# Out-projection tiles in half-row pairs, earlier weight pieces on GpSimd, and a sample product from split pieces

## The chip, the cores and the metric

The kernel runs on one core of a Trainium2 chip. The metric is the device time of one execution in microseconds (us); the median of three executions of the kernel before is 1808.09 us (1805.63 to 1809.71). Engines are named as in the profile: PE is TensorE, PEld its weight loads, DVE VectorE, ACT ScalarE, POOL GpSimd, SP the engine that issues most transfers (DMAs).

## The reference, cut to what matters

One layer of a decoder, for a prompt of 1024 tokens and for 64 sample tokens (8 sequences of 8) that share the weights. Three branches (differential attention, a pooling mixer, memory attention) are merged; then come the steps that this case is about:

```python
    x = x + merged @ w_out
    f, conv_state = conv_ffn(rmsnorm(x, norm2_g), conv_prefix.astype(x.dtype), w_ffn_gate, w_ffn_up,
...
def conv_ffn(h, prefix, w_gate, w_up, conv_w, conv_b, w_down):
    L = h.shape[1]
    g = h @ w_gate
    u = h @ w_up
    ext = jnp.concatenate([prefix, g], axis=1)
    gc = conv_b
    for j in range(CONV_WIDTH):
        gc = gc + conv_w[j] * ext[:, j:j + L]
    f = (jax.nn.gelu(gc) * u) @ w_down
    return f, ext[:, ext.shape[1] - (CONV_WIDTH - 1):]
```

w_out is 1024 x 1024, the gate and up weights 1024 x 2816, w_down 2816 x 1024, and CONV_WIDTH is 3; f is added to x and a last norm follows.

All data are float32. The merge, the projections and the attention ahead of this are the same in both kernels.

## The kernel before, in words

**Numbers in two pieces.** A float32 matrix is split into a high piece (a cast to TensorE's fast float32 form, by ACT, line 109) and a low piece (the rest, by DVE or GpSimd, line 110). A product is then three matmuls: high by high, high by low, low by high. One piece of a weight tile `wA` to `wD` holds 4 x 128 rows by 128 columns; a matmul here is 128x128 by 128x512 and covers 512 tokens.

**The out-projection** (lines 938 to 995) works in two column halves (nb = 0, 1) of 512 columns. In each, the 64 sample rows come first (line 195), then eight tiles of 128 tokens, 24 matmuls a tile (line 187), into the PSUM tag `nat` (two buffers). DVE adds the result to x1 (line 925), ACT squares the sum into the same PSUM tile and sums it (line 926), which frees it. x1 and x1s are loaded for this with DMAs that SP issues (lines 948 and 950). In the second half, a tile is complete: it is normalised (lines 930 and 932, with some small DVE operations of lines 116 to 122) and transposed for the feed-forward part, four 128x128 transposes at a time (line 106, function `put`), into PSUM buffers `tp` and `av` in turn, then split by ACT and DVE.

**Seven products instead of eight.** The feed-forward product of a 256-column weight block with 1024 tokens is done in the manner of Strassen and Winograd: tokens and the rows of x fall in two halves each, and seven products of half size, with sums on both sides, give the result. The token side is B11, B21, B22 (plain) and T1 to T4 (sums and differences). The token halves are the even and the odd tiles: B11 is made of x1[0], x1[2], x1[4], x1[6], and the differences combine x1[2a] with x1[2a+1]. The results therefore go back to token order through strided views (`hv`, `q`).

**The weight blocks.** m runs over 22 blocks, even ones of the gate and odd ones of the up weight. `prep(m)` makes the weight pieces: wA from a11 and a12, wB from s1 and s2, wC from s3 and s4, wD from a22; the sums s1 to s4 are made by GpSimd into buffers `stm` (lines 1080, 1084, 1093, 1097). `products(m)` runs the seven products, 12 matmuls each (line 1108): B11 by wA, T1 by wB, T2 by wB, B21 by wA, T3 by wC, B22 by wC, T4 by wD, into the two halves a and b of a tile `big` (two PSUM banks, two such tiles) and a tile `nat`; ACT copies and DVE adds (line 1124) collect them in SBUF tiles `gu` (six buffers). `prep(m + 1)` is emitted between the products of m. For the sample rows, `sample_ffn` multiplies xs (64 columns wide) with the raw float32 weight: eight products, two rows of the trace each, two at a time side by side in the array (line 1031). The results are transposed (line 106), and in gate blocks convolved (lines 1022 to 1024).

**What sets the order.** The kernel is emitted in program order and then each engine's queue is arranged by a scheduler that works with its own estimates; on the chip each engine runs its queue strictly in that order, and an instruction waits for its operands and for the release of the buffer that it writes. A PSUM tile `big` is released as a whole, both halves. After the feed-forward loop the down projection follows (lines 1174 and on): its matmuls are lines 1221 (prompt) and 1228 (sample, from the split tile `fs`).

Of the kernel before, what the change touches and what calls it, by code (L numbers as in the profile page):

```python
# [32 lines left out]
def hybrid_step(ctx, tc, x_prompt, x_sample, mem_prompt, cache_k, cache_v, page_table, state_pool,  # L33
# [867 lines left out]
    pB_cm = tc.tile_pool(name="pB", bufs=1, reuse_waits="tile")  # L901
    pB = pB_cm.__enter__()
    B11, B21, B22 = [pB.tile([P, 2, 4, 512], F32R, name=f"B{i}") for i in ("11", "21", "22")]

# [9 lines left out]

    with tc.tile_pool(name="p5", bufs=1, reuse_waits="tile") as p5:
        x1 = [p5.tile([P, D], F32, name=f"x1_{t}") for t in range(NT)]
        x1s = p5.tile([TS, D], F32, name="x1s")
        g2b = p5.tile([P, D], F32, name="g2b")
        nc.sync.dma_start(g2b, bc(norm2_g[0], P))
# [13 lines left out]

        def put(Bt, xh, a):
            pt = tpb()
# [5 lines left out]
        raws = {}  # L941
        T1 = T2 = None
        todo, late = [], []
        for nb in range(2):
            n0 = nb * 512
            wf = load_w(cols(w_out, n0))
            if nb == 0:
                nc.sync.dma_start(x1s, x_sample)
                for t in range(NT):
                    nc.sync.dma_start(x1[t], x_prompt[t * P:(t + 1) * P])  # L950
            else:
                raws[0], raws[1] = raw_ffn(0), raw_ffn(1)
            pt = nat()
            mm_s(pt, wf, ms)
            add_sq(x1s, (pt[0:TS], pt[TS:P]), pt[0:TS], TS, NT, nb)
            if nb == 1:
                nc.gpsimd.dma_start(x1s_d, x1s)
                norm2(x1s, TS, NT)
                xs = ap_.tile([P, KT, P], F32, tag="hs", bufs=1, name="xs")
                pt = tpb()  # L960
                for k in range(KT):
                    tr(pt[:, k * TS:(k + 1) * TS], x1s[:, k * P:(k + 1) * P])
                nc.scalar.copy(xs[:, :, 0:TS], pt.rearrange("p (k t) -> p k t", k=KT))
            for i, t in enumerate((0, 2, 1, 3, 4, 6, 5, 7) if nb else range(NT)):
                pt = nat()
# [6 lines left out]
                if i == 3:  # L972
                    T1, T2 = [ap_.tile([P, 2, 4, 512], F32R, tag="act", bufs=4, name=f"T{q}") for q in (1, 2)]
                a = t // 2
                if t % 2 == 0:
                    put(B11, x1[t][:, 0:512], a)
                    put(B21, x1[t][:, 512:D], a)
                    continue
                xa, xb = x1[t - 1], x1[t]
                put(B22, xb[:, 512:D], a)  # L980
                nc.vector.tensor_tensor(xa[:, 0:512], xb[:, 0:512], xa[:, 0:512], op=ALU.subtract)
# [15 lines left out]
    with tc.tile_pool(name="fa", bufs=1, reuse_waits="tile") as fa:  # L997
# [11 lines left out]
        def gu():  # L1009
            return fa.tile([P, T], F32, tag="gu", bufs=6, name=f"gu{uid()}")  # L1010
# [282 lines left out]
```

## Time and profile before

| what | value |
| --- | --- |
| median of three executions | 1808.09 us (1805.63 to 1809.71) |
| the profiled execution | 1810.49 us, its span 1808.7 us |
| mean granted clock of TensorE | 0.987 |
| busy: PE, DVE, ACT, POOL | 1739.5, 899.2, 717.2, 391.7 us |

The span is the time from the first to the last event of the profile. In the order of time a row reads: start, duration from first to last instruction of the group, engine, line, operation, output and inputs, shapes, count, and in brackets the idle time of that engine before it and what ended it. Matmuls are pipelined, so the cadence of a group is the distance of its start to the next start. The granted clock says at what share of its full speed TensorE ran.

### The profile page before, as it was taken

The numbers are of one execution on the slowest core, as the hardware profiler recorded it, in microseconds if no ns is written. First come the engines' busy times: TensorE is split into PE (matmuls) and PEld (weight loads), VectorE is DVE, ScalarE is ACT, GpSimd is POOL, SyncE is SP. The second block draws the span as 40 slices with busy tenths as digits, with TensorE's granted clock in tenths as the row PEclk, the third lists the DMA queues.
The fourth block names the chain that finished last, engine by engine and source line by source line (L and its number), as shares of the span: only waits on it lengthen the run. The fifth ranks groups of instructions, "written<-read, shape, count | busy, mean of one in ns | idle before, by whom it ended". The sixth has DMA issues, their size and how long they took to land.

```text
span 1808.7 us, 22927 instructions
## 1 busy us (share of the span) xinstructions
PE 1739.5 (96%) x8285; PEld 1334.1 (74%) x8285; DVE 899.2 (50%) x1543; ACT 717.2 (40%) x1396; POOL 391.7 (22%) x427
## 2 busy tenths in 40 slices
PE   7999999998999999999989899999999999999997
PEld 5887876764666777767767677777777777888876
DVE  6411134230221666677716676666666666336464
ACT  5321235331222666665413343333333334234343
POOL 1113020301101324112201344444444442000000
PEclk9999999999999999999989899999999999999999
DMA  7441251468565323154432222222222223646563
GB/s 276 139 142 66 83 183 38 135 187 266 195 230 178 96 79 117 56 193 161 145 122 88 49 72 71 71 71 71 71 71 71 71 71 135 226 145 217 197 229 109
DMA packets 137367, 234.74 MB, mean 130 GB/s; under 512 B 25679, under 2 KB 71533, under 8 KB 137253
## 3 DMA queue, kind: packets, MB, share of 16 engines
q1 hardware_dynamic: 122117, 187.16, 32.5%
q0 software_dynamic: 15136, 46.12, 6.8%
q8 instruction: 65, 1.06, 0.2%
q14 instruction: 49, 0.40, 0.1%
HBM read 182.74 MB, written 50.54 MB: 129 GB/s over the span
## 4 chain that ended last, share of the span: by engine, by line
PE 82%; issue 7%; DVE 4%; DMA 3%; ACT 2%; POOL 1%; SPq 1%; POOLq 0%; ACTq 0%; DVEq 0%
PE nat L178 17%; PE big L1108 17%; PE big L1221 10%; PE nat L1108 7%; PE nat L187 6%; PE big L178 4%; PE nat L1221 3%; PE tp L1031 3%; PE tp L106 3%; PE av L106 2%; PE av L804 2%; PE big L774 2%; PE nat L195 2%; PE av L542 1%; PE big L523 1%
## 5 line engine op out<-in xcount | busy, mean ns | idle before, releaser
L178 PE MATMUL nat<-act,hl 128*128 128x512 f32 x1344 | 357.7, 404 | 0.0
L178 PEld LDWEIGHTS nat<-act,hl 128*128 128x128 f32 x1344 | 242.1, 189 | 61.0 <-issue 14.0
L187 PE MATMUL nat<-hl,act 128*128 128x512 f32 x768 | 186.6, 401 | 10.1 <-ACT nat L926 8.3
L1221 PE MATMUL big<-wd,fh 128*128 128x512 f32 x792 | 187.4, 390 | 4.1 <-ACT big L1189 2.5
L187 PEld LDWEIGHTS nat<-hl,act 128*128 128x128 f32 x768 | 146.5, 193 | 42.3 <-ACT nat L926 8.7
L1221 PEld LDWEIGHTS big<-wd,fh 128*128 128x128 f32 x792 | 148.3, 188 | 36.3 <-ACT big L1189 3.4
L1108 PE MATMUL big<-B,wA 128*128 128x512 f32 x528 | 130.5, 395 | 0.1
L110 DVE TENSOR_TENSOR hl<-raw,hl 128x1024 fp32r<-128x1024 f32 x52 | 66.4, 1287 | 123.8 <-ACT hl L109 112.8
L110 DVE TENSOR_TENSOR wd<-wr,wd 128x1024 fp32r<-128x1024 f32 x66 | 84.5, 1282 | 74.1 <-ACT wd L109 68.2
L1108 PEld LDWEIGHTS big<-B,wA 128*128 128x128 f32 x528 | 97.4, 188 | 28.2 <-ACT gu L1133 8.3
L109 ACT CAST wd<-wr 128x1024 fp32r<-128x1024 f32 x66 | 69.3, 1052 | 83.3 <-PE tps L1228 35.3
L110 DVE TENSOR_TENSOR wB<-stm,wB 128x512 fp32r<-128x512 f32 x44 | 50.4, 1147 | 73.6 <-ACT wB L109 73.6
L568 POOL DMA_DIRECT2D gl<-ev x48 | 26.2, 546 | 277.5 <-ACT ev L567 253.2
L567 ACT COPY ev<-nat 128x512 f32<-128x512 f32 x48 | 28.1, 586 | 112.7 <-PE nat L178 106.9
L1108 PE MATMUL nat<-B,wC 128*128 128x512 f32 x264 | 69.9, 399 | 0.0
L109 ACT CAST hl<-raw 128x1024 fp32r<-128x1024 f32 x60 | 62.6, 1053 | 16.3 <-PE nat L178 8.2
L1162 POOL TENSOR_TENSOR gu<-gu,gu 128x1024 f32<-128x1024 f32 x22 | 57.0, 2591 | 52.2 <-DVE gu L1124 22.5
L1221 PE MATMUL nat<-wd,fh 128*128 128x512 f32 x264 | 67.1, 389 | 0.0
L1108 PE MATMUL big<-T,wD 128*128 128x512 f32 x264 | 66.8, 401 | 0.0
L1097 POOL TENSOR_TENSOR stm<-rf,stm 128x512 f32<-128x512 f32 x22 | 28.6, 1299 | 169.8 <-DVE wB L110 169.8
L1108 PE MATMUL big<-T,wC 128*128 128x512 f32 x264 | 64.6, 393 | 0.0
L1108 PE MATMUL nat<-T,wB 128*128 128x512 f32 x264 | 64.1, 390 | 0.0
(419 smaller groups left out, 3080.3 us busy)
## 6 DMA issues: line engine op xcount, KB each, us to landing
wr<-in_w_ffn_down SPq DMA_DIRECT2D x66, 512.0 KB
raw<-in_w_in SPq DMA_DIRECT2D x40, 512.0 KB
kr<-in_cache_k SPq DMA_DIRECT2D x64, 256.0 KB
vr<-in_cache_v SPq DMA_DIRECT2D x64, 256.0 KB
gl<-ev POOLq DMA_DIRECT2D x48, 256.0 KB, 3.0
rf<-in_w_ffn_gate SPq DMA_DIRECT2D x22, 512.0 KB
rf<-in_w_ffn_up SPq DMA_DIRECT2D x22, 512.0 KB
f_d<-gu POOLq DMA_DIRECT2D x22, 512.0 KB, 3.0
```

The lines of the kernel that those rows point to most:

```text
L106: nc.tensor.transpose(out, in_, ident[:n, :n])
L109: nc.scalar.copy(hi, src)
L110: (lo_eng or nc.vector).tensor_tensor(lo, src, hi.bitcast(F32), op=ALU.subtract)
L178: nc.tensor.matmul(out, wf(k, pw)[:, n0:n0 + P], acts[c][ph][:, k, :], start=(k == ks[0] and (pw, ph) == (0, 0)), stop=(k == ks[-1] and (p ...
L187: nc.tensor.matmul(out, acts[c][ph][:, k, o:o + P], wf(k, pw), start=(k == ks[0] and (pw, ph) == (0, 0)), stop=(k == ks[-1] and (pw, ph) = ...
L195: nc.tensor.matmul(out, stack[:, k, :], wf(k, pw), start=(k == ks[0] and pw == 0), stop=(k == ks[-1] and pw == 1))
L774: nc.tensor.matmul(S[:, k0:k0 + n], Qd[:, m, part, qs], Kst[:, m, k0:k0 + n], start=(part == 0), stop=(part == 1))
L804: nc.tensor.matmul(av[:, :P], aT[:, k * P:(k + 1) * P], vn[:, k0 + k], start=(k0 + k == 0), stop=(k0 + k == i))
L1031: nc.tensor.matmul(pt[r:r + TS, 0:256], xs[:, k, 0:TS], raw[k // 4][:, k % 4], start=(k < 2), stop=(k >= 6), tile_position=(0, r))
L1108: nc.tensor.matmul(out, wt[:, pw, k], Bt[:, ph, k], start=(start and k == 0 and (pw, ph) == (0, 0)), stop=(k == 3 and (pw, ph) == (1, 0)), ...
L1162: nc.gpsimd.tensor_tensor(g[i], g[i], gts[i], op=ALU.mult)
L1221: nc.tensor.matmul(banks[i][nb], fh[:, ph, kk, i * P:(i + 1) * P], wh[:, pw, nb * 512:(nb + 1) * 512], start=(k == 0 and (pw, ph) == (0, 0 ...
```

## The change

1. **Token halves in a row.** The two token halves are now tiles 0 to 3 and 4 to 7: B11 is made of x1[0] to x1[3], the differences combine x1[a] with x1[a+4]. The products' results are 512 contiguous tokens, and the strided views are gone.
2. **Out-projection.** Two tiles share one `big` tile, a half each (the sample rows take a half of one too), instead of a `nat` each. Tiles go in the order 0 to 7 in both column halves. The transposes of a tile (`ops_of`) are emitted two tiles behind its projection and take their PSUM buffers from `nat` and from `tp`/`av` in turn, four buffers in all. The four subtractions of a tile pair are all on GpSimd (lines 1115, 1116, 1120, 1121), but for the last pair, where two stay on DVE.
3. **Transfers.** x1s and x1 are loaded ahead of the norm weights g2b and of the first feed-forward weights.
4. **First two weight blocks.** For m = 0 and 1, the low pieces are made by GpSimd, and the sums s1 to s4 in place in the raw weight (lines 1001 to 1004). Their first two products (B11 and B21 by wA) are emitted amid the last transposes.
5. **Sample rows.** Their feed-forward product takes the split weight pieces that the seven products need anyway: 16 matmuls of 128x128 by 128x256 (line 941), with xs and a difference xd split in two pieces side by side. An ACT copy, a DVE addition of 64x512 and one of 64x256 put the four parts together. It runs when wD of its block is ready; its transposes and convolution (lines 932 to 934) follow in the preparation of the next block.
6. The a12 piece is made together with a11, `gu` has five buffers, and two pools lie on the other side of SBUF.

```diff
     def prep(m, early=False):
+        w["a11"] = piece(tA, 0, a11)
+        w["a12"] = piece(tA, 1, a12)
+        yield
+        if early:
+            tD = pair("wD")
+            w["a22"] = piece(tD, 0, a22)
+            nc.gpsimd.tensor_tensor(a22, a21, a22, op=ALU.add)
+            nc.gpsimd.tensor_tensor(a21, a11, a21, op=ALU.subtract)
+            nc.gpsimd.tensor_tensor(a11, a22, a11, op=ALU.subtract)
+            nc.gpsimd.tensor_tensor(a12, a12, a11, op=ALU.subtract)
...
     def sample_ffn(m, w):
+        for i, (n1, n2, st2) in enumerate((("a11", "a12", xs[:, 4:8]), ("s1", "a22", xd))):
             for k in range(KT):
-                nc.tensor.matmul(pt[r:r + TS, 0:256], xs[:, k, 0:TS], raw[k // 4][:, k % 4], start=(k < 2), stop=(k >= 6),
-                                 tile_position=(0, r))
+                nc.tensor.matmul(pt[:, i * 256:(i + 1) * 256].rearrange("p (h x) -> p h x", h=2),
+                                 xs[:, k] if k < 4 else st2[:, k - 4], w[n1][:, :, k] if k < 4 else w[n2][:, :, k - 4],
+                                 start=(k == 0), stop=(k == KT - 1))
...
+        def ops_of(t):
+            if t < 4:
+                put(B11, x1[t][:, 0:512], t)
+                put(B21, x1[t][:, 512:D], t)
+                return
+            a = t - 4
+            ve = nc.vector if t == 7 else nc.gpsimd
+            sums(a, ve)
...
             if nb == 0:
                 nc.sync.dma_start(x1s, x_sample)
                 for t in range(NT):
-                    nc.sync.dma_start(x1[t], x_prompt[t * P:(t + 1) * P])
+                    xl = nc.sync.dma_start(x1[t], x_prompt[t * P:(t + 1) * P])
+                nc.sync.dma_start(g2b, bc(norm2_g[0], P))
...
             for t in range(NT):
+                if t % 2 == 0:
+                    pt2 = big()
+                pt = pt2[:, t % 2]
                 mm_n(pt, wf, macts, t)
...
+                if t >= 2:
+                    ops_of(t - 2)
...
+        pend = [products(0, iter(()), True)]
+        next(pend[0])
+        ops_of(6)
+        next(pp[0])
+        pp[1] = prep(1, True)
+        next(pp[1])
+        pend.append(products(1, prep(2), True))
+        next(pend[1])
+        ops_of(7)
```

What moves on the queues, at three places. First, SP's queue where the out-projection begins. Before (`rf00` is the first feed-forward weight, `x1_0` the first prompt tile):

```order
L159 DMA raw1210_9128<-in_w_out 128x2x512
L911 DMA rf00_9133<-in_w_ffn_gate 128x4x256
L919 DMA g2b_8845<-in_norm2_g 128x1024
L948 DMA x1s_8844<-in_x_sample 64x1024
L950 DMA x1_0_8836<-in_x_prompt 128x1024
```

And of the change:

```order
L159 DMA raw1206_9124<-in_w_out 128x2x512
L1145 DMA x1s_8840<-in_x_sample 64x1024
L1147 DMA x1_0_8841<-in_x_prompt 128x1024
L1147 DMA x1_1_8842<-in_x_prompt 128x1024
L1147 DMA x1_2_8843<-in_x_prompt 128x1024
L1147 DMA x1_3_8844<-in_x_prompt 128x1024
L1147 DMA x1_4_8845<-in_x_prompt 128x1024
L1147 DMA x1_5_8836<-in_x_prompt 128x1024
L1147 DMA x1_6_8837<-in_x_prompt 128x1024
L1147 DMA x1_7_8838<-in_x_prompt 128x1024
L1148 DMA g2b_8839<-in_norm2_g 128x1024
L912 DMA rf00_9298<-in_w_ffn_gate 128x4x256
```

The sample rows moved ahead of the first weight and of the norm weights, which are now behind the eight prompt tiles.

Second, behind the last tile of the out-projection. PE's queue of the change, from the last matmul of tile 7 (`nat`, `tp`, `av` in line 106 are groups of transposes; `wA0` and `wA1` are the first pieces of blocks 0 and 1):

```order
L187 MATMUL big1249_9490<-hl1207_9126,act1069_8001 128x512
L106 MATMUL av1261_9598<-ident_72,x1_5_8836 128x128
L106 MATMUL nat1262_9605<-ident_72,x1_1_8842 128x128 x4
L1043 MATMUL big1264_9623<-B11_8830,wA0_9471 128x512 x2
L106 MATMUL tp1263_9614<-ident_72,x1_5_8836 128x128 x4
L1043 MATMUL big1264_9623<-B11_8830,wA0_9471 128x512 x10
L1043 MATMUL big1264_9623<-B21_8831,wA0_9471 128x512 x12
L106 MATMUL nat1266_9651<-ident_72,x1_6_8837 128x128 x4
L106 MATMUL av1267_9658<-ident_72,x1_2_8843 128x128 x4
L1043 MATMUL big1269_9696<-B11_8830,wA1_9691 128x512
L106 MATMUL nat1268_9667<-ident_72,x1_6_8837 128x128 x4
L1043 MATMUL big1269_9696<-B11_8830,wA1_9691 128x512 x11
```

GpSimd's queue of the change over the same time:

```order
L1115 TENSOR_TENSOR x1_1_8842<-x1_5_8836,x1_1_8842 128x512
L1120 TENSOR_TENSOR x1_4_8845<-x1_4_8845,x1_0_8841 128x512
L1164 DMA x1_d6_8823<-x1_6_8837 128x1024
L1121 TENSOR_TENSOR x1_0_8841<-x1_0_8841,x1_4_8845 128x512
L1116 TENSOR_TENSOR x1_5_8836<-x1_5_8836 128x512
L110 TENSOR_TENSOR wD0_9674<-rf01_9300,wD0_9674 128x512
L1001 TENSOR_TENSOR rf01_9300<-rf00_9298,rf01_9300 128x4x128
L1002 TENSOR_TENSOR rf00_9298<-rf00_9298 128x4x128
L1003 TENSOR_TENSOR rf00_9298<-rf01_9300,rf00_9298 128x4x128
L1115 TENSOR_TENSOR x1_2_8843<-x1_6_8837,x1_2_8843 128x512
L1004 TENSOR_TENSOR rf01_9300<-rf01_9300,rf00_9298 128x4x128
L1116 TENSOR_TENSOR x1_6_8837<-x1_6_8837 128x512
```

Behind these stand the two low pieces of `wB0` with the sum L1120 of x1_5 between them, the operand of the transposes `tp1263` in PE's queue. Before, GpSimd's queue held here only the eight subtractions and a few DMA issues, PE's only transposes and 12 matmuls of block 0.

Third, PE's queue in the loop over blocks, a block before:

```order
L1108 MATMUL big1336_10436<-B11_8830,wA4_10293 128x512 x12
L1108 MATMUL nat1337_10437<-T1_9389,wB4_10309 128x512 x12
L1108 MATMUL big1336_10436<-T2_9390,wB4_10309 128x512 x12
L1031 MATMUL tp1342_10510<-rf50_10289,xs_9175 64x256 x4
L1031 MATMUL tp1342_10510<-rf51_10291,xs_9175 64x256
L1108 MATMUL big1336_10436<-B21_8831,wA4_10293 128x512 x12
L1031 MATMUL tp1342_10510<-rf51_10291,xs_9175 64x256 x3
L1108 MATMUL nat1337_10437<-B22_8832,wC4_10371 128x512 x2
L1108 MATMUL big1336_10436<-T3_9672,wC4_10371 128x512 x12
L1108 MATMUL nat1337_10437<-B22_8832,wC4_10371 128x512 x10
L106 MATMUL av1345_10557<-ident_72,gs5_10519 128x64 x2
L1108 MATMUL big1336_10436<-T4_9673,wD4_10429 128x512 x12
```

A block of the change:

```order
L1043 MATMUL big1320_10457<-B11_8830,wA4_10323 128x512 x12
L1043 MATMUL nat1321_10458<-T1_9360,wB4_10341 128x512 x12
L1043 MATMUL big1320_10457<-T2_9361,wB4_10341 128x512 x12
L106 MATMUL tp1328_10553<-ident_72,gs4_10449 128x64 x2
L106 MATMUL tp1328_10553<-ident_72,st2_10558 128x16 x2
L1043 MATMUL nat1321_10458<-B22_8832,wC4_10376 128x512 x5
L1043 MATMUL big1320_10457<-B21_8831,wA4_10323 128x512 x12
L1043 MATMUL nat1321_10458<-B22_8832,wC4_10376 128x512 x4
L1043 MATMUL big1320_10457<-T3_9621,wC4_10376 128x512 x12
L1043 MATMUL nat1321_10458<-B22_8832,wC4_10376 128x512 x3
L941 MATMUL av1329_10605<-wA5_10478,xs_9163 128x256 x2
L1043 MATMUL big1320_10457<-T4_9622,wD4_10415 128x512 x12
```

The sample rows' matmuls, which stood around the B21 product, stand around the T4 product now (fourteen more follow the last row), and the small transposes moved from before T4 to behind T2. DVE's queue of the change in a gate block, in that same place:

```order
L110 TENSOR_TENSOR wB3_10159<-stm1302_10160,wB3_10159 128x512
L110 TENSOR_TENSOR wB3_10159<-stm1303_10177,wB3_10159 128x512
L932 TENSOR_SCALAR fsv_9817<-es20_10225,cwb_9815 128x64
L932 TENSOR_SCALAR fsv_9817<-es21_10232,cwb_9815 128x64
L933 SCALAR_TENSOR_TENSOR fsv_9817<-es20_10225,cwb_9815,fsv_9817 128x64
L933 SCALAR_TENSOR_TENSOR fsv_9817<-es21_10232,cwb_9815,fsv_9817 128x64
L934 SCALAR_TENSOR_TENSOR fsv_9817<-es20_10225,cwb_9815,fsv_9817 128x64
L934 SCALAR_TENSOR_TENSOR fsv_9817<-es21_10232,cwb_9815,fsv_9817 128x64
L1052 TENSOR_TENSOR gu1300_10134<-gu1300_10134,big1298_10120 128x512
```

The six steps of the sample convolution stood behind the collecting additions of the block and its wD piece; now they stand ahead of the first of these additions (L1052).

370 lines of the change are left out of this document (197 added, 173 removed).

## The prediction

> **What bounds the kernel now.** I read the page's busy shares and its chain that ended last, then the stretches of the changed region (busy time by window), then the order of time of TensorE (PE) inside them. The page first:
>
> ```profile
> PE 1739.5 (96%) x8285; PEld 1334.1 (74%) x8285; DVE 899.2 (50%) x1543; ACT 717.2 (40%) x1396; POOL 391.7 (22%) x427
> ...
> PE 82%; issue 7%; DVE 4%; DMA 3%; ACT 2%; POOL 1%; SPq 1%; POOLq 0%; ACTq 0%; DVEq 0%
> ```
>
> TensorE is the bound, so the change is worth what it takes from TensorE's own queue: its idle time, its slow clock, its instructions. The windows show where idle time and slow clock lie (columns: stretch, length, then busy time and count of PE, PEld, DVE, ACT, POOL, granted clock, DMA share, GB/s):
>
> ```profile
> 907.00:909.00 2.00, 0.22 (x1) 0.00 (x0) 0.00 (x0) 0.00 (x0) 0.00 (x0) 1.00 0.99 280
> ...
> 911.00:913.00 2.00, 0.00 (x0) 0.00 (x0) 0.00 (x0) 0.00 (x0) 0.00 (x0) 0.50 0.99 236
> ...
> 960.00:1014.00 54.00, 51.73 (x257) 41.64 (x256) 37.17 (x90) 16.29 (x40) 9.57 (x12) 1.00 0.22 81
> ...
> 1024.00:1037.00 13.00, 9.46 (x41) 6.85 (x41) 6.95 (x11) 5.41 (x10) 5.59 (x5) 0.50 0.43 3
> ...
> 1050.00:1500.00 450.00, 449.91 (x2050) 339.84 (x2049) 279.48 (x330) 178.98 (x339) 181.63 (x160) 1.00 0.21 71
> ```
>
> There are three places: the start of the out-projection (from 907), the transposes behind it (1014 to 1037), and the feed-forward part, where TensorE never rests and only fewer or shorter instructions help. About 0.2% (3.6 us) is what a measurement of this kernel can tell from no change.
>
> **A. The start of the out-projection.** From the order of time, one row of the chain (DMA), and the page's row of the 256 KB transfers that GpSimd issues:
>
> ```profile
> 901.61 5.61 PE L187 MATMUL nat<-hl,act 128*128 128x512 f32 x24
> ...
> 903.51 9.59 DMA x1s<-in_x_sample
> ...
> 913.19 1.41 DVE L925 TENSOR_TENSOR x1s<-x1s,nat 64x512 f32<-64x512 f32 x2 [8.72 <-DMA x1s<-in_x_sample]
> ...
> 915.54 40.74 PE L187 MATMUL nat<-hl,act 128*128 128x512 f32 x168 [8.32 <-ACT nat L926]
> ...
> 956.11 3.80 PE L195 MATMUL nat<-hl,ms 128*128 128x512 f32 x16
> ```
>
> ```profile
> gl<-ev POOLq DMA_DIRECT2D x48, 256.0 KB, 3.0
> ```
>
> After tile 0's 24 matmuls both `nat` buffers are held; the one with the sample rows frees only when x1s has landed, been added and squared: 8.32 us idle. Then 168 matmuls take 956.11 - 915.54 = 40.57 us; at the cadence of a full-speed matmul, 0.2267 us (12 in 2.72, section D), they are 38.1, so 2.5 went to the half clock. The change leaves the wait (what follows tile 0 still waits for the sample rows' square) but sends x1s ahead of the norm weights, of the first feed-forward weight and of their 1 MB. Its transfer was 9.59 us with all 16 DMA engines full. Bounds: with nothing beside it it lands 3.0 us behind its issue, like `gl<-ev`, and TensorE waits 1 us; or the eight x_prompt transfers behind it share the engines as they do now, and 5 to 6 us stay. I take landing near 907 (3.5 us behind its issue): additions and square, 915.54 - 913.19 = 2.35, put the release at 909.4, and tile 0 ends near 907.1, so some 2.5 us stay idle, shorter than what dropped the clock at 911. New waits: the second tile of each pair shares a PSUM tile with the first and starts only when the first's square is read out (an addition of 0.69, section C, and 2.35 - 1.41 = 0.94 for the square, about 1.65) while 4 to 7 matmuls of the next pair cover 0.9 to 1.6: 1.0 over the four pairs. **A = -8.3 - 2.5 + 2.5 + 1.0 = -7.3** (-9 to -3).
>
> **B. The second column half**, tiles 0 to 7: its first and the next part's first row in the order of time, and the groups of transposes in that stretch (busy, mean ns, idle time before):
>
> ```profile
> 959.75 6.75 PE L187 MATMUL nat<-hl,act 128*128 128x512 f32 x29
> ...
> 1013.98 2.43 PE L1108 MATMUL big<-B,wA 128*128 128x512 f32 x10
> ```
>
> ```profile
> L106 PE MATMUL tp<-ident,x 128*128 128x128 f32 x28 | 4.3, 277 | 0.9 <-DVE x L932 0.5 <-DVE B L110 0.5
> L106 PE MATMUL av<-ident,x 128*128 128x128 f32 x28 | 4.3, 277 | 1.3 <-DVE x L932 0.7 <-DVE T L110 0.6
> ```
>
> 54.2 us for 192 matmuls of 0.2267, 43.5. With the transposes two tiles later the norm (L932) is long done, and four PSUM buffers replace two, so the four waits, 2.2 us, go; two of fourteen groups of transposes move behind tile 7 (54.2 - 43.5 - 2.2 = 8.5 for 14, 0.6 each with their switching). **B = -3.3** (-4 to 0, if the pair waits of A come here too).
>
> **C. Behind tile 7.** Before, fourteen groups of four transposes with 12 product matmuls:
>
> ```profile
> 1030.58 1.09 PE L106 MATMUL av<-ident,x 128*128 128x128 f32 x4 [0.64 <-DVE T L110]
> ...
> 1032.33 0.69 DVE L110 TENSOR_TENSOR T<-av,T 128x512 fp32r<-128x512 f32 x1 [1.04 <-ACT T L109]
> ...
> 1036.76 3.56 PE L1031 MATMUL tp<-rf,xs 128*64 128x256 f32 x16
> ...
> 1040.25 2.34 PE L1108 MATMUL nat<-T,wB 128*128 128x512 f32 x9
> ```
>
> ```profile
> L970 POOL DMA_DIRECT2D x_d<-x x8 | 4.4, 546 | 41.2 <-DVE x L925 37.2 <-DVE ss L930 4.0
> ```
>
> Two PSUM buffers and half clock pace them; 1013.98 to 1040.25 is 26.3 us, with 3.5 for the first sample product. The changed queue has 48 product matmuls here (10.9) and 16 groups of transposes (41 single ones kept TensorE busy for 9.46 at half clock in the row 1024 to 1037, so four take 0.45 at full clock: 7.2): 18.1 of work. Three things add. The last eleven groups follow each other; DVE takes 0.69 for each lower piece, about 0.75 with hand-overs, so +3.3. The T2 group of tile 5 stands near the head of TensorE's queue and waits for the GpSimd sum (L1120), which stands in GpSimd's queue behind thirteen operations and a DMA issue that start when tile 5 is normalised: at 1.28 each (L1097, section D) and 0.55, 17.1 us, while TensorE has about 9.2 us to do: +7.9. Everything behind it in TensorE's queue waits, all 48 matmuls but two. The same wait for tile 6 (eight operations and a DMA issue, 10.8 us, against 6.8) is worth 0 to 4: I take 2. After an idle stretch of that length the clock is 0.50 (the row 911 to 913), which cost 2.5 in A: +2. And GpSimd and DVE hold each other up here (section D's rows): +2.2, between nothing and the 18 of the second rival. Sum 35.5, and 1.9 for the sample product that now comes later, against 26.3 + 36 more matmuls of 0.2267 (8.2) = 34.5. **C = +2.9** (-5 to +8). The casts of the next weights stand in ACT's queue behind the GpSimd sums too, but TensorE is already waiting then.
>
> The clock's rule, told apart from the sum: the Trainium skill (TensorE: Matmul & The Clock Gate, Part 1) says that an idle window of about 3.4 us halves the clock and that as long a busy one restores it; the trace agrees at 911 and at 921. Its remark that transposes do not count as busy also fits 1024 to 1037, where TensorE was busy for 9.46 of 13 us at 0.50; by it the eleven groups at the end would run at half clock, 0.92 each instead of 0.75, 1.9 us more.
>
> **D. The feed-forward loop, 22 weight blocks.** Two blocks (a gate and an up block) before, and what moves:
>
> ```profile
> 1083.48 2.88 PE L1108 MATMUL big<-B,wA 128*128 128x512 f32 x12
> 1086.20 2.88 PE L1108 MATMUL nat<-T,wB 128*128 128x512 f32 x12
> ...
> 1091.74 1.51 PE L1031 MATMUL tp<-rf,xs 128*64 128x256 f32 x10
> ...
> 1096.14 1.08 PE L1031 MATMUL tp<-rf,xs 128*64 128x256 f32 x6
> ...
> 1102.85 0.34 PE L106 MATMUL av<-ident,gs 64*128 64x64 f32 x2
> ...
> 1128.72 2.88 PE L1108 MATMUL big<-B,wA 128*128 128x512 f32 x12
> ```
>
> Starts 1083.48 and 1128.72: 45.24 us a pair, of which 168 matmuls are 38.1 (12 from 1083.48 to 1086.20). Of the other 7.1 some 0.8 are the small transposes (0.27 in an up block, twice that in a gate block), which stay; 6.4 are the sample rows with the gaps around them. Now they are 16 matmuls of 256 columns in the split number form. Nearest rows:
>
> ```profile
> 669.82 0.42 PE L774 MATMUL big<-Kst,Qd 128*128 128x256 f32 x2
> ...
> 670.07 1.79 PE L178 MATMUL nat<-act,hl 128*128 128x512 f32 x7
> ...
> 588.56 0.85 PE L774 MATMUL big<-Kst,Qd 128*128 128x256 f32 x4
> ...
> 589.25 1.10 PE L178 MATMUL nat<-act,hl 128*128 128x512 f32 x4
> ```
>
> Two took 0.25, four with a wait in them 0.69: 0.125 to 0.17 each; half of 0.2267 is the floor, 0.113. I take 0.12 in a run of fourteen. The strided result copies and adds become contiguous, off TensorE's path, at nothing: DVE and ACT are at 62% and 40% in the row 1050 to 1500.
>
> The price is a wait. In gate blocks the sample convolution (three operations on each of two tiles) now stands in DVE's queue ahead of the addition that frees `big` for the T wC product. DVE and GpSimd block each other:
>
> ```profile
> 1093.33 1.28 POOL L1097 TENSOR_TENSOR stm<-rf,stm 128x512 f32<-128x512 f32 x1 [4.30 <-DVE wB L110]
> ...
> 1093.56 1.61 DVE L110 TENSOR_TENSOR wB<-stm,wB 128x512 fp32r<-128x512 f32 x1 [0.31 <-ACT wB L109]
> ...
> 1126.75 2.61 DVE L1022 TENSOR_SCALAR fsv<-es,cwb 128x64 f32<-128x64 f32 x2
> ```
>
> A lower piece took 0.69 alone (1032.33) and 1.61 beside GpSimd, and two small convolution steps 2.61. TensorE has 21 matmuls (4.76) between the second T wB and T wC; with both wB splits, the six steps held by one GpSimd sum, and the addition, DVE ends about 1.07 later, in each gate block. Pair: 38.1 + 32 x 0.12 = 3.84, + 0.8 of small transposes, + four switches of 0.13, + 1.07 = 44.3. **D = -0.95 x 10.5 pairs = -10.0** (-22 with no wait and 0.113; +7 with 0.17).
>
> The rule that speaks against this: the Trainium skill (SBUF — State Buffer, Who interferes with whom) says DVE and GpSimd share one port pair as an exclusive lock, so an instruction with two SBUF inputs waits for the whole of the other's. The 1.61 agrees. Every sum and lower piece moved to GpSimd then costs DVE time as well; it is the second rival below.
>
> **E. Into the down projection.**
>
> ```profile
> 1521.62 1.63 DVE L110 TENSOR_TENSOR fs<-fsv,fs 128x1408 fp32r<-128x1408 f32 x1 [2.93 <-ACT fs L109]
> ...
> 1529.76 3.02 PE L1108 MATMUL big<-T,wD 128*128 128x512 f32 x12
> ...
> 1538.50 2.56 PE L1221 MATMUL big<-wd,fh 128*128 128x512 f32 x10 [1.59 <-DVE fh L110]
> ```
>
> The sample's input fs was ready 6 us before the last product, and matmuls on it filled the gap. Now the last sample product follows that product, its cast and split (1.6) stand ahead of the first fh split, and nine fewer matmuls cover: 2.0 to 4. **E = +2.5.**
>
> **Sum.** -7.3 - 3.3 + 2.9 - 10.0 + 2.5 = -15.2. The profiled execution took 1810.5 us (span 1808.7): 1795.3. The median of the runs shown is 2.4 lower, so the forecast is **1793 us**; its own range, with the terms' bounds mostly independent, 1785 to 1801.
>
> **The rivals.** (1) x1s gains nothing by going first: eight transfers follow within 10 us and the engines are full either way. Against it: 1 MB less stands ahead. A falls to -2: 1798. (2) Slower: GpSimd holds the chip behind tile 7. The norm of tiles 6 and 7 has four small DVE additions and products each; if each waits for one GpSimd operation (1.28) that is 10.2 us, and 23 GpSimd operations that in turn take 1.6, as L1097 did at 1039.33, are 7.6 more; two further restarts at half clock, 5. 1793 + 22.8 = 1816. For it: the rows of D, and
>
> ```profile
> 1017.32 0.84 DVE L119 TENSOR_TENSOR rst<-rsy 128x1 f32<-128x1 f32 x1
> ...
> 1039.33 1.60 POOL L1097 TENSOR_TENSOR stm<-rf,stm 128x512 f32<-128x512 f32 x1 [3.67 <-DVE wB L110]
> ```
>
> Against it: the wide norm step (L932) stays 1.28 beside GpSimd. It decides once the stretch behind tile 7 passes 35 + 15 = 50 us. (3) Faster: no wait at T wC (-11.2) and 0.113 a sample matmul (-2.4): 1779. For it: the wait is one GpSimd operation wide and a little slip hides it.
>
> **Chances.** Forecast 0.56, rival 1 0.12, rival 2 0.19, rival 3 0.13. Faster than 0.2%: 0.53 + 0.08 + 0 + 0.13 = 0.74; no change 0.02 + 0.03 + 0.03 = 0.08; slower 0.01 + 0.01 + 0.16 = 0.18. The range, to 1779 below and 1811 above, leaves out half of rival 3's lower side and most of rival 2.
>
> **What would show it.** In the profile after: the idle time behind tile 0 at 2 to 3 us instead of 8.32 (A); no idle time named DVE B or x L932 among tiles 0 to 7 (B); a TensorE wait on GpSimd L1120 of 6 to 9 us behind tile 7, the clock at 0.50 there, and first T wB 33 to 38 us after tile 7 (C); pairs of 44.0 to 44.6 us with a wait for DVE L1052 near 1 us in gate blocks (D); some 2.5 us more before the down projection's stream (E). A pair of 45.2 or more, or a stretch behind tile 7 of over 50 us, makes the prediction wrong.

## The result and the profile after

The changed kernel takes 1818.83 us (median; 1814.67 to 1819.67), the kernel before beside it 1807.48: a ratio of 1.0057, 95% interval 1.0046 to 1.0069. It is slower by 0.6%, where 0.8% faster was forecast. The profiled execution has a span of 1817.6 us against 1808.7. TensorE stays the bound:

```profile
PE 1741.1 (96%) x8289; PEld 1355.3 (75%) x8289; DVE 882.1 (49%) x1547; ACT 725.2 (40%) x1397; POOL 428.1 (24%) x448
```

TensorE in the order of time, from the out-projection to the first T wB product (columns as before: start, duration, engine, line, operation, tiles, shape, count, idle time before and what ended it):

```profile
900.05 5.61 PE L187 MATMUL big<-hl,act 128*128 128x512 f32 x24
909.07 36.28 PE L187 MATMUL big<-hl,act 128*128 128x512 f32 x144 [3.41 <-ACT big L1095]
945.19 1.07 PE L195 MATMUL big<-hl,ms 128*128 128x512 f32 x4
...
955.96 6.64 PE L187 MATMUL big<-hl,act 128*128 128x512 f32 x28 [0.62 <-ACT big L1095]
...
1002.72 0.66 PE L106 MATMUL nat<-ident,x 128*128 128x128 f32 x4 [2.14 <-POOL x L1120]
...
1003.24 7.32 PE L187 MATMUL big<-hl,act 128*128 128x512 f32 x24
1010.40 0.27 PE L106 MATMUL av<-ident,x 128*128 128x128 f32 x1
...
1018.74 1.12 PE L106 MATMUL tp<-ident,x 128*128 128x128 f32 x4 [7.17 <-POOL x L1120]
1019.51 7.55 PE L1043 MATMUL big<-B,wA 128*128 128x512 f32 x22
...
1031.96 1.12 PE L106 MATMUL nat<-ident,x 128*128 128x128 f32 x4 [3.79 <-POOL x L1120]
1032.73 7.98 PE L1043 MATMUL big<-B,wA 128*128 128x512 f32 x23
...
1047.49 0.96 PE L1043 MATMUL nat<-T,wB 128*128 128x512 f32 x3
```

The wait of 8.32 us is 3.41 now, the waits for DVE among tiles 0 to 7 are gone, and three waits for the GpSimd sum L1120 (2.14, 7.17, 3.79) are new. The clock falls behind each of the long ones (the eighth number is the granted clock):

```profile
910.00:920.00 10.00, 10.00 (x35) 7.97 (x34) 0.69 (x1) 0.76 (x3) 0.00 (x0) 0.74 0.83 322
...
1010.00:1020.00 10.00, 2.83 (x15) 2.26 (x14) 2.20 (x5) 4.07 (x9) 9.92 (x9) 0.70 0.00 0
...
1030.00:1040.00 10.00, 8.04 (x25) 6.54 (x26) 1.24 (x2) 0.59 (x1) 3.17 (x3) 0.66 0.01 2
```

From 1010 to 1020 GpSimd is busy for 9.92 of 10 us and TensorE for 2.83. In the loop over blocks, and in the down projection:

```profile
1128.40 2.96 PE L1043 MATMUL big<-B,wA 128*128 128x512 f32 x12
1131.21 2.91 PE L1043 MATMUL nat<-T,wB 128*128 128x512 f32 x12
...
1143.16 3.02 PE L1043 MATMUL big<-T,wC 128*128 128x512 f32 x12 [0.74 <-DVE gu L1052]
...
1173.46 2.96 PE L1043 MATMUL big<-B,wA 128*128 128x512 f32 x12
...
1528.01 3.02 PE L1043 MATMUL big<-T,wD 128*128 128x512 f32 x12
...
1534.80 0.73 PE L1281 MATMUL big<-wd,fh 128*128 128x512 f32 x2 [3.29 <-ACT fh L109]
...
1542.02 2.96 PE L1281 MATMUL big<-wd,fh 128*128 128x512 f32 x12
...
1603.46 2.96 PE L1281 MATMUL big<-wd,fh 128*128 128x512 f32 x12
1606.26 1.56 PE L1281 MATMUL nat<-wd,fh 128*128 128x512 f32 x6
```

The first long run on fh and the same twelve matmuls of the down projection before:

```profile
1541.81 2.88 PE L1221 MATMUL big<-wd,fh 128*128 128x512 f32 x12
...
1604.60 2.88 PE L1221 MATMUL big<-wd,fh 128*128 128x512 f32 x12
1607.32 1.52 PE L1221 MATMUL nat<-wd,fh 128*128 128x512 f32 x6
```

A pair of blocks is 1173.46 - 1128.40 = 45.06 us against 45.24. But twelve matmuls of the down projection, whose instructions and order the change does not touch, take 2.80 us to the next start where they took 2.72. That was in no term. From the starts of all matmuls, the median from one to the next is 0.234 on B11 and B21, 0.235 on B22 and 0.232 to 0.235 on fh, against 0.227 in all of these before; T1 and T2, which lie where they lay, stay at 0.227.

Where the time of the two profiled executions went, term by term (equal work: the 36 product matmuls that moved ahead of the first T wB, and the first sample product that moved behind it, are set off against each other; nine of the sample's matmuls that the change does later are put to E):

| stretch | forecast | measured | how |
| --- | --- | --- | --- |
| ahead of tile 0 | 0 | -1.6 | 900.05 for 901.61 |
| A, up to tile 0 of the second half | -7.3 | -2.2 | 55.91 for 58.14 |
| B, tiles 0 to 7 | -3.3 | +0.2 | 54.4 for 54.2 |
| C, behind tile 7 | +2.9 | +5.0 | 37.1 + 2.3 for 26.3 + 8.2 |
| D, the blocks | -10.0 | -3.1 | 478.2 for 481.4 |
| E, from T wD of the last block (1528.01, before 1529.76) to the first long run on fh (1542.02, before 1541.81) | +2.5 | +4.0 | 14.0 + 2.0 for 12.0 |
| the rest of the down projection | 0 | +6.6 | 273.5 for 266.9 |
| sum | -15.2 | +8.9 | spans |

### The profile page after: what moved, and what is told of

Read it like the earlier page. It is cut to its first block, busy times and chain, and to the rows that moved or that the text cites. A ratio compares the mean times of both kernels' runs of the same rounds, so it can differ in the third digit from the quotient of the medians.

```text
span 1817.6 us, 23008 instructions
## 1 busy us (share of the span) xinstructions
PE 1741.1 (96%) x8289; PEld 1355.3 (75%) x8289; DVE 882.1 (49%) x1547; ACT 725.2 (40%) x1397; POOL 428.1 (24%) x448
## 5 line engine op out<-in xcount | busy, mean ns | idle before, releaser
L1281 PE MATMUL big<-wd,fh 128*128 128x512 f32 x792 | 193.3, 397 | 5.7 <-ACT fh L109 3.3
L1043 PE MATMUL big<-B,wA 128*128 128x512 f32 x528 | 135.5, 406 | 0.0
L187 PE MATMUL big<-hl,act 128*128 128x512 f32 x384 | 94.8, 407 | 4.8 <-ACT big L1095 4.7
L187 PE MATMUL nat<-hl,act 128*128 128x512 f32 x384 | 92.0, 398 | 1.8 <-DVE act L110 1.0
L187 PEld LDWEIGHTS big<-hl,act 128*128 128x128 f32 x384 | 74.4, 196 | 23.1 <-ACT big L1095 7.4
L187 PEld LDWEIGHTS nat<-hl,act 128*128 128x128 f32 x384 | 72.8, 191 | 18.1 <-DVE act L110 1.8
L1043 PE MATMUL nat<-B,wC 128*128 128x512 f32 x264 | 74.2, 404 | 0.0
L110 DVE TENSOR_TENSOR wB<-stm,wB 128x512 fp32r<-128x512 f32 x40 | 45.5, 1139 | 53.4 <-ACT wB L109 53.4
L110 DVE TENSOR_TENSOR wA<-rf,wA 128x512 fp32r<-128x512 f32 x40 | 52.6, 1336 | 29.1 <-ACT wA L109 29.1
```

The source lines that it names most:

```text
L110: (lo_eng or nc.vector).tensor_tensor(lo, src, hi.bitcast(F32), op=ALU.subtract)
L187: nc.tensor.matmul(out, acts[c][ph][:, k, o:o + P], wf(k, pw), start=(k == ks[0] and (pw, ph) == (0, 0)), stop=(k == ks[-1] and (pw, ph) = ...
L1043: nc.tensor.matmul(out, wt[:, pw, k], Bt[:, ph, k], start=(start and k == 0 and (pw, ph) == (0, 0)), stop=(k == 3 and (pw, ph) == (1, 0)), ...
L1281: nc.tensor.matmul(banks[i][nb], fh[:, ph, kk, i * P:(i + 1) * P], wh[:, pw, nb * 512:(nb + 1) * 512], start=(k == 0 and (pw, ph) == (0, 0 ...
```

## The experiments

Two theories for the slower matmuls came first: where the tiles begin, or on which side of SBUF they lie. The change moved two pools to the right side, `pB` with the B tiles and `fb` with fh. In the kernel's memory map (bytes within a partition) their tiles now begin at 180192 (B11) and 190432 (fh0), 32 bytes past a multiple of 64. Before it was 138176 and 147392, both multiples of 64.

**e1_aligned**, the changed kernel with 32 bytes more in both pools:

```diff
     B11, B21, B22 = [pB.tile([P, 2, 4, 512], F32R, name=f"B{i}") for i in ("11", "21", "22")]
+    pB.tile([P, 8], F32, name="padB")
...
         gfb = fb.tile([P, D], F32, name="gfb")
+        fb.tile([P, 8], F32, name="padF")
```

> The changed kernel with 32 bytes of padding in the two pools on the right side of SBUF, nothing else; the queues stay as they are. In the changed kernel B11, B21, B22 and the fh tiles begin 32 bytes past a multiple of 64, with the padding at a multiple of 64. Theory 'start address': the matmuls that read them take 0.233 us instead of 0.2267 for that reason alone, 792 on B tiles and 1056 on fh tiles, so (0.2333 - 0.2267) x 1848 = 12 us go: 1806 to 1807 us, cadence 0.227 on all of them. Rival 'side': the place at the other end of SBUF, or other engines' traffic there, slows them: no change, 1818 us, cadence 0.233.

Measured: ratio 1.0001 (0.9992 to 1.0010). The whole loss is gone with 32 bytes, 0.56% or 10 us. The profile of that kernel, the down projection again:

```profile
1599.90 2.88 PE L1283 MATMUL big<-wd,fh 128*128 128x512 f32 x12
1602.62 1.52 PE L1283 MATMUL nat<-wd,fh 128*128 128x512 f32 x6
```

2.72 for twelve, and 0.227 to 0.228 on the B tiles. A pair of blocks of this kernel, for later:

```profile
1102.26 2.91 PE L1044 MATMUL big<-B,wA 128*128 128x512 f32 x12
...
1138.78 3.03 PE L1044 MATMUL big<-T,wC 128*128 128x512 f32 x12 [0.87 <-DVE gu L1053]
...
1147.12 2.91 PE L1044 MATMUL big<-B,wA 128*128 128x512 f32 x12
```

**b2_shifted**, the reverse: in the kernel before, `pB.tile([P, 8], F32)` ahead of the B tiles and `fb.tile([P, 8], F32)` ahead of fr.

> The kernel before with the same tiles moved by 32 bytes on the left side where they are, nothing else. Theory 'start address': 12 us more, about 1820 us, cadence 0.233 on the B and fh matmuls and 0.227 on the others. Rival 'side': no change, 1808 us.

Measured: 1.0065 (1.0052 to 1.0078), 0.234 to 0.235 on both. The side of SBUF is out.

```profile
1600.66 2.96 PE L1223 MATMUL big<-wd,fh 128*128 128x512 f32 x12
1603.46 1.56 PE L1223 MATMUL nat<-wd,fh 128*128 128x512 f32 x6
```

**e2_b_only**, e1 without `padF`.

> The changed kernel with the padding in the pool of the B tiles alone; the fh tiles stay 32 bytes past a multiple of 64. Theory 'start address': the feed-forward products come to 0.227, the down projection stays at 0.233: 792 x 0.0066 = 5 us less than the changed kernel, about 1813 us. Rival: no change or all of it.

Measured: 1.0041 (1.0028 to 1.0055). The products are back at 0.227, the down projection stays at 0.232. So both count, B as the moving operand and fh as the stationary one; B is worth 0.16% (3 us, less than the 5 expected), fh 0.40% (7 us).

**b3_shift64**, b2 with `[P, 16]` for `[P, 8]`, was meant as a control.

> The kernel before with the B and fh tiles moved by 64 bytes on the left side, nothing else; a control for the run with 32 bytes. Theory 'start address': they still begin at a multiple of 64, so no change, within 0.15%, cadence 0.227. Rival 'any move': slower, as with 32 bytes (1.0065).

Measured: 1.0053 (1.0038 to 1.0068), fh at 0.234. The theory as it was put, a multiple of 64, fell. What all fast cases so far have in common is the distance of the two operands: weight pieces and T tiles begin at 960 in 1024, and so do B and fh before and in e1.

**f4_left32** moves the other operand, with everything else on the left side, in the changed kernel:

```diff
+    cp.tile([P, 8], F32, name="padC")
     ident = cp.tile([P, P], F32, name="ident")
```

> The changed kernel with 32 bytes of padding ahead of everything on the left side of SBUF: the weight pieces, the down-projection weights and T1 to T4 move, the B and fh tiles stay where the change put them. The control with 64 bytes was slower (1.0053), so a multiple of 64 is not the condition. Theory 'relative': what counts is how the starts of the two operands of a matmul stand to each other (in all fast cases both begin at 960 in 1024; now both begin at 992): the 10 us come back, about 1808 us, cadence 0.227 on the B and fh matmuls. Rival 'absolute': a start at 960 in 1024 is needed by itself: now T and the weights are off too, 3% on nearly all matmuls from there on, 1830 us or more.

Measured: 1.0004 (0.9994 to 1.0013). B11 and fh lie where the change put them, and the loss is gone:

```profile
1602.65 2.88 PE L1282 MATMUL big<-wd,fh 128*128 128x512 f32 x12
1605.37 1.52 PE L1282 MATMUL nat<-wd,fh 128*128 128x512 f32 x6
```

It is the distance. **f2_shift128**, **f2_shift256** and **f2_shift512** ask for its period (b2 with `[P, 32]`, `[P, 64]` and `[P, 128]`).

> The kernel before with the B and fh tiles moved by 128 bytes. If the relation repeats every 128 bytes (or 64 of 128 is what counts): no change, 0.227, ratio 1.000. If it repeats at 256 bytes or more: slower as with 32 and 64 bytes, ratio 1.005, 0.231 to 0.235.

> The kernel before with the B and fh tiles moved by 256 bytes. What counts is the distance of the two operands' starts; 32, 64 and 128 bytes are slow. If it repeats every 256: ratio 1.000 and 0.227; if every 512 or more: 1.005 and 0.231 to 0.235.

> The kernel before with the B and fh tiles moved by 512 bytes. The fast pieces of one tile lie 512 bytes apart from one another already (stationary blocks of 128 columns), so a period of 512 at most is expected: ratio 1.000 and 0.227. If it is slow, the period is longer and the reading of the relation is wrong.

Measured: 1.0046 (1.0032 to 1.0060), 1.0007 (0.9998 to 1.0016) and 1.0000 (0.9991 to 1.0009); the matmuls at 0.232 to 0.234, 0.227 and 0.227. So distances of 32, 64 and 128 bytes are slow and 0, 256 and 512 fast: within what was tried, it repeats every 256 bytes.

Then the places where the terms missed: first one edit on the aligned kernel (e3), then one edit each on e3. A difference of two ratios is uncertain by about 0.18%, as each of them is by 0.13%.

**e3_sums_dve**, two of the four subtractions of every tile pair on DVE, as before the change (the sum L1120 is line 1121 in the kernels with padding):

```diff
-            ve = nc.vector if t == 7 else nc.gpsimd
+            ve = nc.vector
```

> The aligned changed kernel with two of the four subtractions of every tile pair on DVE, as they were before the change; the early weight sums and low pieces stay on GpSimd. Theory 'GpSimd sums hold TensorE': the three waits for L1120 (2.1, 7.2 and 3.8 us) and the half-clock matmuls behind them (1.7, 2.4 and 2.6) go: 12 to 18 us less than the aligned kernel, about 1792 us. Rival 'the weight pieces hold it': the waits move to the pieces of wA1, wB0 and wC0, which stay on GpSimd, and less than 5 us are gained, about 1803 us.

Measured: 0.9968 (0.9955 to 0.9980), 0.33% or 6 us less than e1, between the two. TensorE behind tile 7:

```profile
1013.91 1.01 PE L1044 MATMUL big<-B,wA 128*128 128x512 f32 x2 [2.73 <-ACT big L1096]
...
1018.83 1.22 PE L1044 MATMUL big<-B,wA 128*128 128x512 f32 x2 [3.91 <-POOL wA L110]
...
1023.87 1.12 PE L106 MATMUL nat<-ident,x 128*128 128x128 f32 x4 [3.82 <-DVE x L1121]
```

The three waits for GpSimd's sums became three others: for a square in ACT's queue, for a low piece of wA on GpSimd, and for a sum on DVE whose tile is normalised late. The stretch from tile 7's last matmul to the first T wB is 33 us instead of 37, in e1 as in the changed kernel.

**e6_low_dve**, on e3, takes the low pieces of the first two blocks from GpSimd too:

```diff
-            split(tl[:, i, 0], tl[:, i, 1], src, nc.gpsimd if early else None)
+            split(tl[:, i, 0], tl[:, i, 1], src)
```

> The kernel e3 with the low pieces of the first two weight blocks on DVE, as before the change; the four sums of each block in place stay on GpSimd. Theory 'GpSimd queue': the wait of 3.9 us for a low piece of wA on GpSimd goes and the stretch behind tile 7 shrinks by 4 to 8 us (ratio about 0.993). Rival 'DVE is the bound there': DVE is late then with the norm and the lower pieces, and the time stays or rises by up to 4 us.

Measured: 0.9927 (0.9914 to 0.9940), 0.41% or 7 us less than e3. TensorE's waits there are down to 1.5 and 2.7, and the stretch is 26 us:

```profile
1013.85 1.20 PE L1044 MATMUL big<-B,wA 128*128 128x512 f32 x2 [1.54 <-ACT wA L109]
...
1017.76 1.12 PE L106 MATMUL nat<-ident,x 128*128 128x128 f32 x4 [2.71 <-DVE x L1121]
```

GpSimd's queue of sums and low pieces together held TensorE: without the sums (e3) a part of the wait moved to the low pieces, and without both (e6) some 11 us of the stretch are gone. The low pieces alone were not taken away.

**e5_sample_nat**, on e3, for term A:

```diff
-            pt2 = big()
-            mm_s(pt2[:, 1], wf, ms)
-            add_sq(x1s, (pt2[0:TS, 1], pt2[TS:P, 1]), pt2[0:TS, 1], TS, NT, nb)
+            pt = nat()
+            mm_s(pt, wf, ms)
+            add_sq(x1s, (pt[0:TS], pt[TS:P]), pt[0:TS], TS, NT, nb)
```

> The kernel e3 (aligned, two of four subtractions on DVE) with the sample rows of the out-projection in a nat buffer instead of a half of a big tile, so that tile 2 can run while x1s is on its way. Theory for term A: the wait for x1s (2.5 to 4.0 us) and the half clock behind it (2.5 to 3.6 us) are what A missed; both go, and the two waits of 0.6 to 0.7 at the second half as well: 4 to 7 us less than e3 in proportion to before (ratio about 0.994). Rival: the wait is that for the prompt tile's own transfer, which comes behind x1s, and stays: within 1 us of e3.

Measured: 0.9945 (0.9932 to 0.9957), 0.23% or 4 us less than e3, at the lower end of what was expected. One wait of 0.89 is left, and 128 matmuls behind it run at full clock:

```profile
903.91 9.24 PE L187 MATMUL big<-hl,act 128*128 128x512 f32 x40
914.03 29.81 PE L187 MATMUL big<-hl,act 128*128 128x512 f32 x128 [0.89 <-ACT big L1096]
```

**e8_conv_late**, on e3, for the wait in D:

```diff
-            flush_s()
             yield
+            flush_s()
             tD = pair("wD")
```

> The kernel e3 with the transposes and the convolution of the sample rows one step later in the preparation of the next block, behind the addition that frees the tile for T wC. Theory for term D: ten waits of 0.8 to 0.9 us in gate blocks go: 7 to 9 us less (ratio about 0.992). Rival: the delay moves to the next addition or to the wD product: less than 2 us.

Measured: 0.9918 (0.9905 to 0.9931), 0.50% or 9 us less than e3; of the waits for the DVE addition one of 0.2 us is left, and a pair of blocks is 1142.01 - 1098.13 = 43.88 us where it was 44.86:

```profile
PE big L1044 <- DVE gu L1053: 0.2, 1, 0.2
```

```profile
1098.13 2.91 PE L1044 MATMUL big<-B,wA 128*128 128x512 f32 x12
...
1142.01 2.91 PE L1044 MATMUL big<-B,wA 128*128 128x512 f32 x12
```

**e7_flush_early**, on e3, for term E: in the last block, `flush_s()` behind the second product.

> The kernel e3 with the transposes of the last block's sample rows behind its second product instead of behind its last. Theory for term E: the split of fs is done before the last product again, its matmuls fill the gap ahead of the down projection, and 3 to 4 us go (ratio about 0.995). Rival: the gap is set by the split of fh and its transfer alone: less than 1 us.

Measured: 0.9951 (0.9938 to 0.9965), 0.17% or 3 us less than e3, at the edge of what can be told; the profile shows the cause removed. Matmuls on fs fill the gap again:

```profile
1523.28 1.17 PE L1292 MATMUL tps<-wd,fs 128*128 128x512 f32 x4
...
1529.07 2.58 PE L1285 MATMUL big<-wd,fh 128*128 128x512 f32 x10 [1.44 <-DVE fh L110]
```

**e9_all**: e3 with the edits of e5, e6, e7 and e8.

> All four edits on top of e3: sample rows in nat, low pieces of the first two blocks on DVE, early transposes of the last sample rows, convolution one step later. If they act in different places, as theory has it, their gains add up: 0.9968 - 0.0023 - 0.0041 - 0.0017 - 0.0050 = 0.984 of the time before, about 1780 us. Rival 'they share a cover' (the same slack is used twice, above all DVE behind tile 7): 0.988 or more.

Measured: 1779.02 us, 0.9834 (0.9821 to 0.9848). They add up.

**e11_ob**: e9 with `p3.tile([P, 96], F32)` ahead of the ob tiles, which are the moving operand of branch projections and lie 128 bytes off (151104 against 11200, the distance in 256) in both kernels of this case.

> The kernel e9 with 384 bytes of padding ahead of the ob tiles of the branch projections, which in all kernels so far begin at 576 in 1024 while the weights begin at 960 (128 apart in 512) and whose matmuls have a median cadence of 0.232 against 0.227 for those on act. Theory 'relative': 0.227 for them too, 384 x 0.005 = 2 us less than e9, ratio about 0.9825. Rival: they are slow for another reason (their switches between PSUM tiles): no change.

Measured: 1777.85 us, 0.9823 (0.9808 to 0.9838). The time is not told apart from e9's, but the matmuls are: 0.227 for 0.232 at the median. Twelve of them in e9, then in e11:

```profile
813.27 2.95 PE L178 MATMUL big<-ob,hl 128*128 128x512 f32 x12
```

```profile
810.71 2.88 PE L178 MATMUL big<-ob,hl 128*128 128x512 f32 x12
```

So this version is 1.8% faster than the kernel before, and every edit but the ob padding only takes back something that the change brought with it: a distance between tiles, two duties of GpSimd, one PSUM buffer and two places in the order cost more than the rest of the change gained.

## Why the prediction was wrong, point by point

**The missing term.** The prediction costed what every engine does and waits for, and gave the move of two pools to the other side of SBUF no line at all. The 32 bytes that came with this move are worth 0.56%, 10 us (e1, f4), by making some 1850 matmuls 2 to 3.5% longer. With them taken out the kernel stands at 1.0001: the forecast of 15 us would still have been wrong. Neither of the two signs that were to make the prediction wrong came (a pair of 45.2 or more, over 50 us behind tile 7; they were 45.06 and 37): both look where the sum had terms, and the down projection, where 6.6 us went, had none outside E.

**A** failed at "some 2.5 us stay idle, shorter than what dropped the clock". The release moved as described, and 3.41 us stayed, and the clock fell: 0.74 from 910 to 920. 144 matmuls took 36.12 us instead of 32.6. But the limit itself was wrong too. In e1 a shorter wait, from 903.76 to 906.21, does the same:

```profile
906.21 1.50 PE L187 MATMUL big<-hl,act 128*128 128x512 f32 x4 [2.45 <-ACT big L1096]
```

```profile
903.51:906.92 3.41, 0.96 (x5) 0.62 (x4) 1.85 (x3) 0.72 (x2) 0.00 (x0) 1.00 1.02 402
906.92:910.33 3.41, 3.19 (x9) 2.00 (x8) 0.20 (x1) 0.72 (x2) 0.00 (x0) 0.50 1.02 407
```

These stretches are not chosen freely. In all 17 traces of this case every change of the granted clock (247 of them) lies a whole number of 3.413 us behind the start of its clock record, to within 0.004 us: the clock is granted window by window. The window in which the wait fell was busy for 0.96 of 3.41 us (0.28), and the next one ran at half clock, though the matmuls had started again. From 850 us on, a full-clock window with a busy share of 0.40 or less was always followed by one at half clock, none of 0.49 or more was, and between 0.42 and 0.48 both occur; a half-clock window needed 0.85 or more to be followed by full clock, and 0.81 was too little. Earlier in the kernel some windows with a larger share lost the clock too (near 140 us shares of 0.71 to 1.00), and why is not shown. The prediction read its limit off a wait of 8.32 us, as if only a wait that long counted; even the 2.5 us that it forecast would have been enough if they fell into one window, and where the windows lie against the wait differs from trace to trace. The Trainium skill (TensorE: Matmul & The Clock Gate, Part 1) says that the clock falls after at least one idle window of about 3.4 us: the window's length agrees, but here a window that was only partly idle was enough, and the measurement decides. The 0.89 of e5 dropped nothing.

**B** failed at one place. The four waits for DVE and the norm went, as said, but the T2 transposes of tile 4 stand inside this stretch, and their GpSimd sum (2.14 us late) and the half clock behind it (24 matmuls in 7.16 instead of 5.44) cost 3.9. The prediction put the GpSimd queue's cost to C alone.

**C** was right about the first wait on L1120: 7.9 us were forecast from GpSimd's queue, and 7.17 came. For the second it took 2, by the same queue, and 3.79 came, in good part by another way. In GpSimd's queue a sum of tile 7 (L1116) stands ahead of that L1120, and it had to wait for DVE's sum (L1115), which needs tile 7 normalised. In that norm one DVE step on 128x1 numbers lasted 5.38 us instead of 0.15, beside four low pieces that GpSimd ran from 1021.70 to 1026.70:

```profile
1021.34 5.38 DVE L119 TENSOR_TENSOR rst<-rsy 128x1 f32<-128x1 f32 x1
```

```profile
1021.70 2.50 POOL L110 TENSOR_TENSOR wC<-rf,wC 128x512 fp32r<-128x512 f32 x2
1024.17 2.53 POOL L110 TENSOR_TENSOR wA<-rf,wA 128x512 fp32r<-128x512 f32 x2
1029.42 1.26 POOL L1116 TENSOR_TENSOR x<-x 128x512 f32<-128x512 f32 x1 [2.73 <-DVE x L1115]
1030.65 1.26 POOL L1120 TENSOR_TENSOR x<-x,x 128x512 f32<-128x512 f32 x1
```

By an estimate from these rows, 2.73 of the 3.79 us, the time that GpSimd stood idle ahead of L1116, are this step's. The clock fell twice, not once: 22 and 23 matmuls took 7.4 and 7.8 to the next start instead of 5.0 and 5.2, 5 us instead of 2. The first T wB was 37 us behind tile 7, within the 33 to 38 that were named, which owes something to luck: the eleven groups of transposes at the end took 0.63 each, not 0.75. The remark that transposes do not count as busy, by which they would run at half clock, did not hold: the window from 1041.43 to 1044.84 has transposes alone, busy for 2.81 of 3.41 us, and the clock stayed at 1.00 in it and in the next. e3 and e6 show that GpSimd's sums and low pieces hold this stretch, and that the casts and squares behind them are the next wait, which the prediction had set aside with "TensorE is already waiting then".

**D** has its price of a matmul right (medians 0.119 and 0.120 for 256 columns; 0.12 was taken) and the wait at T wC in its place, but smaller: ten waits of 8.0 us in all in the aligned kernel, where 1.07 in every pair was taken. What was mis-sized is "four switches of 0.13". In the aligned kernel a pair is 1147.12 - 1102.26 = 44.86: less 38.1, 3.84, 0.8 and its wait of 0.87, 1.25 are left for the switches instead of 0.52. Behind the sample product, the small transposes or the wait, the next five to ten matmuls come at up to 0.236, the first at times at 0.33, before the cadence is 0.227 again. The row 588.56, which the prediction read as a run with a wait in it, shows no wait: its four starts are 0.22, 0.13 and 0.22 apart. The 0.73 over 10.5 pairs are some 8 us, the wait was 3 us cheaper, and the missing term takes 2 to 3 us more. (The lower bound of -22 should have been -23.6 by the two terms that rival 3 names.)

**E** came out at its upper bound, 4.0: TensorE waited 3.29 for the first fh and the nine matmuls on fs came later. e7 gives about 3 us back.

**The rivals.** The slower side was reached, but its largest part, the 32 bytes, was in no rival. The second rival's mechanism did come, at three of its eight steps: 1.27 and 1.14 us in the norm of tile 6 and the 5.38 above in that of tile 7, 7.3 us more than 0.15 each, where 10.2 were put. Its rule, the port pair that DVE and GpSimd lock against each other (the Trainium skill, SBUF — State Buffer, Who interferes with whom), agrees: a step with two SBUF inputs stood until GpSimd's run of four operations had ended. With three low pieces beside it (e3) the same step took 3.96 us, and with the low pieces on DVE (e6) no 128x1 step behind tile 7 took over 0.16. What the prediction held against this rival was a misreading: the wide norm step "stays 1.28 beside GpSimd", but before the change it never ran beside a GpSimd operation, and where it did in the changed kernel it took 2.32 (at 1006.39).

## What to carry to other kernels

When a change moves buffers, compare the start addresses of the two operands of each matmul before and after, and keep them a multiple of 256 bytes apart; a cadence of 0.232 to 0.235 in place of 0.227 on untouched instructions is the sign. Sum the queue of the slowest engine up to the operand that TensorE waits for, and then look at what stands second there, since removing the first wait alone gave 6 of 13 us. Add what a small DVE step loses beside a run of GpSimd operations. Put the half clock into the sum for idle time of some 2 us within one 3.4 us window, and not only for a wait that lasts until the clock falls.

## What the runs showed of the hardware that was not expected

Matmuls of 128x512 in a long run follow each other at 0.227 us if the moving and the stationary operand begin at a distance that is a multiple of 256 bytes within a partition, and at 0.231 to 0.235 if it is 32, 64 or 128 bytes off, whichever of the two is moved (f4 against e1). Why is not shown. Other distances were not tried, and nothing smaller than 32 bytes.

Behind a wait or matmuls of another shape, some matmuls come at 0.23 to 0.236 even when aligned, and then the run settles at 0.227; the misaligned ones stay there. It is not at every switch: T wB behind B wA comes at 0.227 from the first in the kernel before. Why is not shown.

The clock is granted in windows of 3.413 us, and what counts is how much of one window TensorE was busy (A, above). So a wait of 2.45 us dropped it in e1, and one of 2.14 in the changed kernel (its window from 1000.44 on was busy for 0.37), though both were over when it fell; the 1.44 in e7's rows did not (0.58). The clearest case is a wait of 2.24 or 2.25 us for GpSimd near 585 us, well ahead of the change and the same in all 17 traces. In the seven where two windows shared it so that neither held more than 1.42 us of it, the clock stayed; in the ten where one held 1.61 or more, it fell. Which of the two a kernel gets is chance.

A 128x1 step of DVE lasted 5.38 us instead of 0.15, until four GpSimd operations in a row had ended (C, above).
